# All tiles at multiples of 64 bytes in a partition, and projection pieces of 432, 448 or 480 columns

## The chip, the core and the metric

The kernel runs on one core of a Trainium2 chip. The time is what the device takes for one execution of the whole program, in microseconds (us); lower is better. TensorE (PE in the profile) multiplies, with its weight loads listed apart as PEld; VectorE (DVE), ScalarE (ACT) and GpSimd (POOL) do the rest, and SyncE (SP) issues the DMAs.

## What is computed

Two transformer blocks of two layers each, over 256 tokens with 1024 features, in float32:

```
for l in range(2):      # first block
    x = x + 0.5 * swiglu(rms_norm(x, ffn1_norm[l]), w_gate, w_up, w_down)     # 1024 -> 2816 -> 1024
    h = rms_norm(x, mix_norm[l])
    proj = h @ w_in[l]                       # split: GLA, FOX attention, SSD, short convolution
    x = x + concatenate([gla, fox, ssd, sconv]) @ w_out[l]
    x = x + 0.5 * swiglu(rms_norm(x, ffn2_norm[l]), ...)
for l in range(2):      # second block: the same, but
    proj = h @ w_in_2[l]                     # split: NSA (compressed, selected, window) and MOBA heads
    x = x + concatenate([o_nsa, o_moba]) @ w_out_2[l]
return rms_norm(x, norm_final_2)
```

## The kernel before

**Precision.** Every dense product is made of float32r products: each operand is split exactly into a first and a second part (`hi`, `lo` of a weight, `xhi`, `xlo` of the tokens), and three of the four partial products are summed in PSUM. `weights` (L320 to L335) loads a piece of a weight matrix into a tile `raw`, ACT copies it into `hi` (L332), DVE subtracts (L333) and writes `lo`.

**Which operand streams.** A product has a stationary operand, loaded by LDWEIGHTS, and a moving one, whose columns stream past it. There are four kinds of dense product.

- `gemm_T` (feed-forward gate and up, and projection pieces that come out transposed): stationary are 128 columns of `hi` or `lo`, moving is `xs`, the tokens' two parts side by side. For each 128 columns there is one matmul of 512 columns (`hi`) and one of 256 (`lo`), in two PSUM banks in turn.
- Feed-forward down, in `ffn`: the same pair of 512 and 256 columns, but moving is a tile `hT` (22 of them, made by L524 and L525), in four PSUM banks in turn.
- `w_out`: three matmuls of 256 columns, moving `yhi`, `ylo`, `yhi`.
- `project`: tokens as rows. Stationary are 128 columns of `xs`, moving is a row of the weight piece, `hi`, `lo` and `hi` again through `mm3`; so each piece has twice as many `hi` as `lo` products. Its pieces are 436, 434 and 434 columns wide in the first block (`W1`) and six times 474 in the second (`W2`). With 8 blocks of features, 2 halves of the tokens and 3 products, a piece is 48 matmuls.

**Order.** A phase of feed-forward runs its pieces one after the other. In a mixing phase `drive` puts the mixers' small float32 products and transposes between the dense products: it keeps a clock `self.clk`, which `mm` moves on by columns / 2400 (four times that for float32), and a mixer goes on when that clock has reached the time at which it expects its input. So the width of a piece enters the order in which TensorE's instructions are written. `pieces` asks for a piece's weights one piece ahead.

**Where tiles lie.** The pools place tiles one after another in each partition, every tile at the next multiple of 32 bytes. In the built program these are the starts modulo 64 bytes:

```
tile                      before                         after
x, xs, cst (ident)        0                              0
raw, hi, lo               32                             0
hT, g, h, sq, ss          32                             0
yhi, ylo                  32 in mix1, 0 in mix2          0
pj                        32                             0
s2, sm, p, pT             32 in mix1, 0 in mix2 (sm: both)   0
row k of hi, lo in project:
  436 columns             32, 48, 0, 16                  0 (448 columns)
  434 columns             32, 40, 48, 56                 0 (432 columns)
  474 columns             32, 8, 48, 24                  0 (480 or 448 columns)
```

The tile `gf` of 32 bytes is what puts the pools behind it at 32; `prm`, `ms` and `r` and the rows of `pj` (1304 and 2844 floats for each half of the tokens) shift others.

Of the kernel before, what the change touches and what calls it, by code (L numbers as in the profile page):

```python
# [21 lines left out]
# widths of the pieces in which the input projections are computed  # L22
# with tokens as rows; the other columns come out transposed, 256 at a time
W1 = [436, 434, 434]
W2 = [474] * 6
IN1, IN2 = sum(W1), sum(W2)
NB1 = 9
# NSA heads in the order that pairs a head of group 0 with one of group 1
POS = [0, 4, 1, 5, 2, 6, 3, 7]

# [20 lines left out]
def _consts():  # L51
    """Masks, triangles and rope tables: they depend on shapes alone."""
# [38 lines left out]
def _pack(widths, w):  # L91
    """[1024, sum(widths)] -> flat, one [128, 8, width] block after the other."""
    w = w.reshape(8, 128, -1).transpose(1, 0, 2)
    out, o = [], 0
    for n in widths:
        out.append(w[:, :, o:o + n].reshape(-1))
        o += n
    return np.concatenate(out)
# [6 lines left out]
def layout(inp):  # L105
    """Lays the inputs out for the chip: slices, transposes, copies."""
    a = {k: np.asarray(v) for k, v in inp.items()}
    f32 = np.float32
# [11 lines left out]
    for l in range(2):  # L120
# [9 lines left out]
        out[f"wi{l}"] = _pack(W1, np.concatenate([lr, bf, cdt, bq, bk, bv, av, ag], 1))  # L130
# [66 lines left out]
class Body:  # L197
# [5 lines left out]
    def run(self, ctx, phases, final):  # L203
# [10 lines left out]
        # x transposed, in two halves of the features: [128, (block of 128 features, token)]  # L214
        self.x = [self.cst.tile([128, 4, 256], F32, name=f"x{n}") for n in range(2)]
        C = self.cst.tile([128, CW], F32, name="cst")
# [6 lines left out]
        # keeps the array busy, and its clock up, until the first operands are there  # L223
# [22 lines left out]
        self.gf = self.cst.tile([128, 8], F32, name="gf")  # L246
# [47 lines left out]
    def params(self, ph, cut=None):  # L294
        """Loads a block's parameters, in two parts if asked to: then returns the second's load."""
        key = ph[2], ph[3]
        if key in self.pars:
            return
        fields, w = (_P1, PW1) if ph[2] == "p1" else (_P2, PW2)
        p, src = self.prm.tile([128, max(PW1, PW2)], F32, name="prm"), self.a[f"{ph[2]}_{ph[3]}"]  # L300
        self.pars[key] = {n: p[:, o:o + k] for n, (o, k) in fields.items()}
        self.nc.sync.dma_start(p[:, :cut or w], src[:, :cut or w])
        return lambda: self.nc.sync.dma_start(p[:, cut:w], src[:, cut:w])
# [14 lines left out]
    def weights(self, src, nk, n, parts=1, then=None):  # L318
        """A piece of a weight matrix and its exact split into two float32r parts."""
# [34 lines left out]
    def behind(self):  # L354
        """Matrix products traced in it are issued behind the dense ones traced so far."""
        return self.tc.issue_after(self.last_mm) if self.last_mm is not None else nullcontext()

    def drive(self, dense, mixers):
        """Interleaves the dense products with the mixers' steps. A generator yields before a product
        that has to wait: how much of other products to put before it, the name of what it needs, or  # L360
        "@" for one of the places among the attentions in progress."""
# [28 lines left out]
    def rrow(self, pool, r):  # L390
        """r [128 tokens, 2] as a row over the 256 tokens, on every partition."""
# [9 lines left out]
    def norm(self, k):  # L401
        """A block of 128 features of x times the next norm's gain, split in two."""
# [5 lines left out]
    def sumsq(self, n):  # L408
        """Sums of x's squares over half the features, but for the sum over the partitions."""
# [13 lines left out]
    def rfin(self):  # L423
        """(mean of x's squares + eps) ** -0.5: [128 tokens, 2]"""
        nc = self.nc
        ms = self.wk.tile([128, 2], F32, name="ms")
        r = self.wk.tile([128, 2], F32, name="r")
# [9 lines left out]
    def x_done(self, n):  # L437
        """Half of x's features are final."""
        if self.nxt:
            self.sumsq(n)  # L440

    def x_last(self, n, b):
        """A block of the last x: its squares join the sums; turned to tokens as rows by a product with
        the last norm's gains on a diagonal."""
# [22 lines left out]
    def gemm_T(self, ps, ws, k):  # L467
        """256 columns of a weight matrix, through 128 of its rows: in PSUM, for each block of 128 columns,
        the products with the tokens' first and second parts side by side."""
# [8 lines left out]
    def evac_T(self, out, ps, R, eng):  # L478
        """out [128, 2 * 256] = the sums of the parts, times the tokens' factors."""
# [78 lines left out]
    def pieces(self, make):  # L558
        """Runs the dense pieces, each a pair (load, run); a piece's weights are asked for one ahead."""
# [7 lines left out]
    def project(self, w, widths, c, half, box):  # L567
        """Half of the rows of a piece of the projection with tokens as rows."""
# [24 lines left out]
    def project_T(self, w, c, R, box):  # L593
        """256 columns of the projection, transposed: box[c] [128, 512] = (block of 128, token)."""
# [13 lines left out]
    def w_out(self, i, kq, n, box, last):  # L608
        """x += y @ w_out, through the rows kq of w_out, for half the columns."""
# [37 lines left out]
    def finish(self, y, k0, nk, g):  # L647
        """Columns of y [128, 2, nk * 128] into the transposed, split operand of w_out."""
# [13 lines left out]
    def rms(self, y, n, d, scale=1.0, eps=EPS):  # L662
        """(mean of squares over the last d + eps) ** -0.5 of y [128, n * d] -> [128, n]."""
# [15 lines left out]
    def sigm(self, out, x):  # L679
        """1 / (1 + exp(-x)) = exp(-ln(1 + exp(-x)))"""  # L680
# [5 lines left out]
    def attn2(self, qT, kT, v, po, first=True, last=True, guard=True, gate=None):  # L686
        """Two heads' causal softmax(q k) v over 256 tokens, transposed, onto po [2 * 64, 256] in PSUM.
        qT[h], kT[h]: [d, 256], one of them negated; v[h][t]: [128, 64]; gate: [128, (h, t)] factors of the rows."""
# [40 lines left out]
    def pv2(self, po, v, a, b, first, last):  # L729
        """po [2 * 64, 256] += v[h]^T P[h]^T; a: keys 0..127 by (h, 256 queries), b: keys 128.. by  # L730
        (h, the last 128 queries)."""
# [7 lines left out]
    def finish_T(self, y, k0, n, mat, d, src=None, wait=2.5):  # L739
        """rms norm over d rows of the transposed y [128, n * 256] (PSUM src, else in place), with the  # L740
        gains, into the split operand of w_out."""
# [12 lines left out]
        # one Newton step for the root  # L754
# [44 lines left out]
    def logs(self):  # L799
        """log-sigmoids: of GLA's gate and FOX's forget logit, and -softplus of SSD's step."""  # L800
# [33 lines left out]
    def gla(self, c0, B):  # L834
        """c0: columns of v and the output gate in pj; B[0], B[1]: transposed q and k."""
# [24 lines left out]
        # v of each head, zero in the columns of the pair's other head  # L860
# [79 lines left out]
    def fox(self, c0):  # L940
# [21 lines left out]
        # the running sums of the log forget gates, next to q and k  # L962
# [39 lines left out]
    def conv(self, x, acc, j, taps, bias):  # L1002
        """acc[:, j] = causal convolution of x[:, j] along the tokens; taps[-1] is the newest."""
# [117 lines left out]
    def compress(self, l):  # L1121
        nc, P, pj, C = self.nc, self.P, self.pj, self.C
        mm = self.mm
        # the windows of k and v plus their positions, transposed: [(parity, d), (l / 2, g, n)]
# [32 lines left out]
        # hidden = window @ w1: four partial sums, on four groups of 32 partitions (g, n)  # L1157
# [61 lines left out]
    def pairT(self, c, n, dst, scale=None):  # L1219
        """n blocks of 128 columns of pj from c, transposed to [128, 256] each."""  # L1220
# [42 lines left out]
    def nsa_cmp(self):  # L1263
        """The compressed branch: all heads at once, columns (head, n)."""
# [34 lines left out]
    def nsa_pair(self, p):  # L1299
        """The compressed branch's values, and the selected and window branches: over 256 tokens both see  # L1300
        all that is not in the future."""
# [61 lines left out]
```

## Time and profile before

| | us |
|---|---|
| median of 3 runs (lowest, highest) | 2036.2 (2035.51, 2037.14) |
| profiled execution, span from its first to its last instruction | 2034.5 |
| TensorE busy in it | 2017.6 |
| VectorE, ScalarE, GpSimd busy | 1623.0, 1226.2, 417.8 |

No other time of the profiled execution is recorded than its span, which lies 1.7 us under the median. Matmuls are pipelined and their ends are modelled, so TensorE's busy share says little of its pace. The pace is read from the starts: the time from one matmul's start to the next one's, or a stretch of the chain of waits that is TensorE alone, divided by its count of matmuls.

### The profile page before, as it was taken

What the parts mean: (1) busy time and instruction counts of PE and PEld (TensorE: products, weight loads), DVE (VectorE), ACT (ScalarE), POOL (GpSimd) and SP (SyncE); (2) the same over time, 40 slices, a digit from 0 to 9 for tenths busy, and PEclk for the clock granted to TensorE, in tenths of its full rate; (3) what the DMA queues carried; (4) which work ended last, traced back from release to release, by engine and by line L of the source; (5) the groups of instructions that cost most, each with busy time, mean ns of one, the idle gap of its engine ahead of it and who ended that gap; (6) DMA issues with size and microseconds to landing.
All of it is one profiled execution on the core that took longest, in us unless ns stands there. A gap on an engine that the chain in (4) does not pass through costs nothing.

```text
span 2034.5 us, 32098 instructions
## 1 busy us (share of the span) xinstructions
PE 2017.6 (99%) x12052; PEld 1769.3 (87%) x12052; DVE 1623.0 (80%) x3140; ACT 1226.2 (60%) x2711; POOL 417.8 (21%) x313
## 2 busy tenths in 40 slices
PE   9999999999999999999999999999999999999998
PEld 7888889888888888988888887898888888789887
DVE  7976888995897688899589766889868976688974
ACT  6655666664665566666466545766556654566653
POOL 2320121330221013132022111023203211103320
PEclk9999999999999999999999999999999999999999
DMA  7655425555555542655555556255555555624552
GB/s 277 210 195 175 155 87 200 198 184 194 190 187 181 197 143 73 221 197 184 192 192 188 181 190 216 80 170 194 187 194 186 187 185 180 217 84 173 194 182 73
DMA packets 54300, 360.88 MB, mean 177 GB/s; under 512 B 6272, under 2 KB 6656, under 8 KB 16768
## 3 DMA queue, kind: packets, MB, share of 16 engines
q1 hardware_dynamic: 54144, 358.83, 50.7%
q8 instruction: 94, 1.54, 0.3%
q14 instruction: 62, 0.51, 0.1%
HBM read 357.76 MB, written 1.05 MB: 176 GB/s over the span
## 4 chain that ended last, share of the span: by engine, by line
PE 92%; issue 3%; DVE 3%; ACT 1%; POOL 0%; DMA 0%; DVEq 0%; POOLq 0%; SPq 0%
PE ps L343 90%; PE ps L347 2%; DVE lo L333 1%; DVE s L1011 1%; DVE xs L405 0%; ACT p L703 0%; DMA raw<-gu 0%; DVE x L633 0%; POOL s L1023 0%; PE ps L395 0%; PE ps L431 0%; ACT hi L332 0%; DVE p L701 0%; POOL g L486 0%; DVE s L756 0%
## 5 line engine op out<-in xcount | busy, mean ns | idle before, releaser
L333 DVE TENSOR_TENSOR lo<-raw,hi 128x512 fp32r<-128x512 f32 (+2 forms) x1336 | 1059.1, 824 | 233.7 <-ACT hi L332 220.2
L343 PE MATMUL ps<-xs,hi 128*128 128x512 f32 x3104 | 1088.2, 393 | 3.4 <-DVE xs L405 3.4
L332 ACT ACTIVATE hi<-raw 128x512 fp32r<-128x512 f32 (+2 forms) x1336 | 751.3, 620 | 270.4 <-PE ps L343 147.3
L343 PE MATMUL ps<-xs,lo 128*128 128x256 f32 x3104 | 875.7, 282 | 0.9 <-DVE lo L333 0.9
L343 PEld LDWEIGHTS ps<-xs,hi 128*128 128x128 f32 x3104 | 584.6, 188 | 126.5 <-DVE xs L405 3.9
L343 PEld LDWEIGHTS ps<-xs,lo 128*128 128x128 f32 x3104 | 588.0, 190 | 2.7 <-DVE lo L333 1.6
L343 PE MATMUL ps<-hT,hi 128*128 128x512 f32 x1408 | 494.7, 393 | 0.0
L486 POOL TENSOR_TENSOR g<-g,R 128x512 f32<-128x512 f32 x176 | 296.1, 1684 | 635.3 <-DVE g L484 614.8
L343 PE MATMUL ps<-hT,lo 128*128 128x256 f32 x1408 | 398.2, 283 | 0.0
L343 PEld LDWEIGHTS ps<-hT,hi 128*128 128x128 f32 x1408 | 264.4, 188 | 61.1
L343 PEld LDWEIGHTS ps<-hT,lo 128*128 128x128 f32 x1408 | 264.7, 188 | 0.0
L484 DVE TENSOR_TENSOR g<-ps,g 128x256 f32<-128x256 f32 x352 | 147.3, 421 | 63.3 <-ACT g L483 63.2
L483 ACT ACTIVATE g<-ps 128x256 f32<-128x256 f32 x352 | 132.9, 379 | 91.6 <-PE ps L343 91.3
L343 PE MATMUL ps<-hi,xs 128*128 128x474 f32 (+2 forms) x576 | 182.0, 381 | 0.0
L522 ACT ACTIVATE h<-g 128x256 f32<-128x256 f32 x176 | 73.7, 419 | 178.5 <-POOL g L486 178.4
L524 ACT ACTIVATE hT<-h 128x256 fp32r<-128x256 f32 x176 | 73.3, 418 | 82.2 <-DVE h L523 82.2
L343 PEld LDWEIGHTS ps<-hi,xs 128*128 128x128 f32 x576 | 108.0, 188 | 14.6 <-issue 2.3
L343 PE MATMUL ps<-lo,xs 128*128 128x474 f32 (+2 forms) x288 | 107.2, 372 | 0.0
L523 DVE TENSOR_TENSOR h<-h,g 128x256 f32<-128x256 f32 x176 | 78.3, 447 | 15.3 <-ACT h L522 15.3
L415 POOL TENSOR_TENSOR sq<-sq 128x512 f32<-128x512 f32 x12 | 18.4, 1534 | 324.7 <-ACT sq L414 324.7
L434 POOL TENSOR_TENSOR r<-ms,cst 128x2 f32<-128x2 f32 x13 | 11.2, 862 | 328.6 <-DVE ms L433 328.6
L525 DVE TENSOR_TENSOR hT<-h,hT 128x256 fp32r<-128x256 f32 x176 | 73.4, 419 | 1.9 <-ACT hT L524 1.9
(214 smaller groups left out, 1540.5 us busy)
## 6 DMA issues: line engine op xcount, KB each, us to landing
raw<-gu SPq DMA_DIRECT2D x174, 1024.0 KB, 4.8
raw<-wd SPq DMA_DIRECT2D x80, 1024.0 KB, 4.8
raw<-wj SPq DMA_DIRECT2D x24, 948.0 KB, 4.8
raw<-wb SPq DMA_DIRECT2D x18, 1024.0 KB, 4.8
raw<-wo SPq DMA_DIRECT2D x12, 1024.0 KB, 5.0
raw<-wd SPq DMA_DIRECT2D x16, 512.0 KB, 3.3
raw<-cw SPq DMA_DIRECT2D x8, 1024.0 KB, 4.9
raw<-wi SPq DMA_DIRECT2D x8, 868.0 KB, 4.5
```

What stands on the lines that cost most here:

```text
L332: nc.scalar.activation(hi[:, c], raw[:, c], AF.Copy)
L333: nc.vector.tensor_tensor(lo[:, c], raw[:, c], hi[:, c].bitcast(F32), op=OP.subtract)
L343: return self.nc.tensor.matmul(out, w, x, **kw)
L347: self.nc.tensor.transpose(out, x, self.ident)
L483: nc.scalar.activation(o, ps[b][:, 256:512], AF.Copy)
L484: nc.vector.tensor_tensor(o, ps[b][:, 0:256], o, op=OP.add)
L486: eng.tensor_tensor(o2, o2, R[:, None, :].to_broadcast([128, 2, 256]), op=OP.mult)
L522: self.last_silu = nc.scalar.activation(h, g[:, 0:256], AF.Silu).ins
L523: nc.vector.tensor_tensor(h, h, g[:, 256:512], op=OP.mult)
L524: nc.scalar.activation(hT[c][:, 0], h, AF.Copy)
L525: nc.vector.tensor_tensor(hT[c][:, 1], h, hT[c][:, 0].bitcast(F32), op=OP.subtract)
L1011: nc.vector.scalar_tensor_tensor(a[:, s:], p[:, :256 - s], taps[len(taps) - 1 - s], a[:, s:], op0=OP.mult, op1=OP.add)
```

## The change

Widths are rounded so that every tile, and every row of a weight piece in `project`, starts at a multiple of 64 bytes. The zero columns at the end (8 in `W1`, 4 more than before in `W2`) are multiplied like the others and written to `pj`, where nobody reads them. All comments and docstrings are gone as well, so line numbers are lower or higher by a few (L343 becomes L350).

```diff
-W1 = [436, 434, 434]
-W2 = [474] * 6
+W1 = [448, 432, 432]
+W2 = [480] * 5 + [448]
+def _up(n):
+    return -(-n // 16) * 16
...
-        out[f"wi{l}"] = _pack(W1, np.concatenate([lr, bf, cdt, bq, bk, bv, av, ag], 1))
+        pad = np.zeros((DM, IN1 - 1304), f32)
+        out[f"wi{l}"] = _pack(W1, np.concatenate([lr, bf, cdt, bq, bk, bv, av, ag, pad], 1))
...
-        C = self.cst.tile([128, CW], F32, name="cst")
+        C = self.cst.tile([128, _up(CW)], F32, name="cst")
...
-        self.gf = self.cst.tile([128, 8], F32, name="gf")
+        self.gf = self.cst.tile([128, 16], F32, name="gf")[:, :8]
...
-        p, src = self.prm.tile([128, max(PW1, PW2)], F32, name="prm"), self.a[f"{ph[2]}_{ph[3]}"]
+        p, src = self.prm.tile([128, _up(max(PW1, PW2))], F32, name="prm"), self.a[f"{ph[2]}_{ph[3]}"]
...
-        ms = self.wk.tile([128, 2], F32, name="ms")
-        r = self.wk.tile([128, 2], F32, name="r")
+        ms = self.wk.tile([128, 16], F32, name="ms")[:, :2]
+        r = self.wk.tile([128, 16], F32, name="r")[:, :2]
```

In the feed-forward phases no instruction moves. In `mix2` the other widths shift `drive`'s clock, and TensorE's order changes in some places. The first is in the compressed branch, where `raw` and `s` are its products with the window weights, `cst,pj` are transposes, and `hi,xs` and `lo,xs` the projection. Before:

```order
L343 MATMUL ps<-hi,xs 128x474
L343 MATMUL ps<-raw,s_12354 32x256 x8
L347 MATMUL ps<-cst,pj 128x128 x8
L343 MATMUL ps<-cst,s_12422 128x128 x4
L343 MATMUL ps<-hi,xs 128x474
```

After, on TensorE at the same place:

```order
L350 MATMUL ps<-raw,s_12351 32x256 x8
L350 MATMUL ps<-hi,xs 128x480
L350 MATMUL ps<-lo,xs 128x480
L350 MATMUL ps<-hi,xs 128x480
L350 MATMUL ps<-cst,s_12413 128x128 x4
L350 MATMUL ps<-hi,xs 128x480
L350 MATMUL ps<-lo,xs 128x480
L350 MATMUL ps<-hi,xs 128x480 x2
L350 MATMUL ps<-lo,xs 128x480
L350 MATMUL ps<-hi,xs 128x480
L354 MATMUL ps<-cst,pj 128x128 x8
```

One group of float32 work between two dense products has become three. The second place is the transposes of the attention's probabilities `p` in the last projection piece. Before:

```order
L343 MATMUL ps<-hi,xs 128x474
L347 MATMUL ps<-cst,p 128x128
L343 MATMUL ps<-lo,xs 128x474
L347 MATMUL ps<-cst,p 128x128 x5
L343 MATMUL ps<-hi,xs 128x474 x2
```

After, on TensorE at the same place:

```order
L350 MATMUL ps<-hi,xs 128x448
L350 MATMUL ps<-lo,xs 128x448
L354 MATMUL ps<-cst,p 128x128 x4
L350 MATMUL ps<-hi,xs 128x448
L354 MATMUL ps<-cst,p 128x128 x2
```

The dense products between the transposes stand one product later. Over the whole program the dense and the other products follow one another, change of kind counted, 284 times before and 292 times after.

## Rows read from the trace of the kernel before

**Rows 1.** The page: busy time of TensorE, the granted clock in 40 slices, and the shares of the chain of waits by engine.

```profile
PE 2017.6 (99%) x12052; PEld 1769.3 (87%) x12052; DVE 1623.0 (80%) x3140; ACT 1226.2 (60%) x2711; POOL 417.8 (21%) x313
...
PEclk9999999999999999999999999999999999999999
...
PE 92%; issue 3%; DVE 3%; ACT 1%; POOL 0%; DMA 0%; DVEq 0%; POOLq 0%; SPq 0%
```

**Rows 2.** The longest waits of TensorE: who waited for whom, us in total, times, longest.

```profile
PE ps L343 <- POOL s L1023: 5.4, 2, 2.7
PE ps L343 <- DVE xs L405: 3.4, 1, 3.4
...
PE ps L343 <- DVE lo L333: 0.9, 2, 0.5
```

**Rows 3.** The chain of waits in the first feed-forward phase, once in its gate and up products (`gemm_T`), once in its down products: start, length, instructions.

```profile
23.29 110.82 PE ps L343 x639
...
134.11 61.56 PE ps L343 x351
```

**Rows 4.** Instructions of TensorE in order of time, in the gate and up products: start and length in us.

```profile
60.23 0.39 PE L343 MATMUL ps<-xs,hi 128*128 128x512 f32 x1
60.45 0.28 PE L343 MATMUL ps<-xs,lo 128*128 128x256 f32 x1
...
61.27 0.39 PE L343 MATMUL ps<-xs,hi 128*128 128x512 f32 x1
```

**Rows 5.** The same in the down products; the rows left out are their `lo` products.

```profile
139.68 0.40 PE L343 MATMUL ps<-hT,hi 128*128 128x512 f32 x1
...
140.03 0.39 PE L343 MATMUL ps<-hT,hi 128*128 128x512 f32 x1
...
140.38 0.40 PE L343 MATMUL ps<-hT,hi 128*128 128x512 f32 x1
...
140.73 0.40 PE L343 MATMUL ps<-hT,hi 128*128 128x512 f32 x1
...
141.09 0.39 PE L343 MATMUL ps<-hT,hi 128*128 128x512 f32 x1
```

**Rows 6.** The same in `w_out`, first in `mix1`, then in `mix2`; between the two rows of each lie eight matmuls of 256 columns.

```profile
318.52 0.28 PE L343 MATMUL ps<-ylo,hi 128*128 128x256 f32 x1
...
319.58 0.28 PE L343 MATMUL ps<-ylo,hi 128*128 128x256 f32 x1
...
1330.23 0.28 PE L343 MATMUL ps<-ylo,hi 128*128 128x256 f32 x1
...
1331.31 0.28 PE L343 MATMUL ps<-ylo,hi 128*128 128x256 f32 x1
```

**Rows 7.** The same in `project`, at a width of 434 and of 474; between the two rows of each lie eleven matmuls.

```profile
209.10 0.36 PE L343 MATMUL ps<-lo,xs 128*128 128x434 f32 x1
...
211.48 0.36 PE L343 MATMUL ps<-lo,xs 128*128 128x434 f32 x1
...
1246.07 0.38 PE L343 MATMUL ps<-lo,xs 128*128 128x474 f32 x1
...
1248.66 0.37 PE L343 MATMUL ps<-lo,xs 128*128 128x474 f32 x1
```

**Rows 8.** Groups of TensorE instructions by shape: count, busy us, mean ns of one, idle time before them. PEld rows are weight loads, of `hi` at 32 bytes and of `xs` at 0.

```profile
L343 PE MATMUL ps<-xs,hi 128*128 128x512 f32 x3104 | 1088.2, 393 | 3.4 <-DVE xs L405 3.4
...
L343 PEld LDWEIGHTS ps<-xs,hi 128*128 128x128 f32 x3104 | 584.6, 188 | 126.5 <-DVE xs L405 3.9 <-issue 1.2
L343 PE MATMUL ps<-hT,hi 128*128 128x512 f32 x1408 | 494.7, 393 | 0.0
...
L343 PE MATMUL ps<-hi,xs 128*128 128x474 f32 x384 | 125.9, 389 | 0.0
L343 PEld LDWEIGHTS ps<-hi,xs 128*128 128x128 f32 x576 | 108.0, 188 | 14.6 <-issue 2.3
...
L343 PE MATMUL ps<-hi,xs 128*128 128x434 f32 x128 | 37.7, 365 | 0.0
```

**Rows 9.** One VectorE operation of the attention, on `p`, by shape: in the first layer's `mix1` (195 to 331 us) and `mix2` (1212 to 1346 us).

```profile
L714 DVE TENSOR_SCALAR p<-p,sm 128x256 f32<-128x256 f32 x4 | 1.4, 346 | 0.0
...
L714 DVE TENSOR_SCALAR p<-p,sm 128x256 f32<-128x256 f32 x24 | 8.7, 362 | 0.3
```

**Rows 10.** TensorE in order of time around one group of float32 products in `mix2`.

```profile
1230.30 0.37 PE L343 MATMUL ps<-hi,xs 128*128 128x474 f32 x1
1230.60 1.07 PE L343 MATMUL ps<-raw,s 128*32 128x256 f32 x16
1231.60 0.49 PE L343 MATMUL ps<-hi,xs 128*128 128x474 f32 x1
1231.93 0.38 PE L343 MATMUL ps<-lo,xs 128*128 128x474 f32 x1
```

**Rows 11.** The chain of waits in `mix1` from 251 to 272 us: two of its longest pieces, and its last.

```profile
260.69 2.70 DVE s L1011 x5
...
264.10 2.41 DVE lo L333 x4
...
269.73 2.39 POOL s L1023
```

## The prediction

> **What bounds the kernel now.** I read the page first. TensorE is busy 99% of the span, its granted clock is in the top tenth in all 40 slices (the upper level, 2.4 GHz), and the chain of waits is TensorE for 92% [rows 1]. A reader might stop there, but ends of matmuls are modelled, so the next view is TensorE's waits: beyond 3.4 us at the start there are two of up to 2.7 us in `mix1` and two of 0.5 us [rows 2]. Hardly 10 us of 2034.5 are waits, so only two things can move the time: the pace at which products follow one another, and the order in which kinds of product follow.
>
> The pace is read from starts. In gate and up, 639 matmuls of the chain take 110.82 us, 173.4 ns each [rows 3]. Half have 512 columns, half 256, on average 384, which at 2.4 GHz is 160.0; so 13.4 ns come on top. In down, the same pair of shapes takes 61.56 us for 351, or 175.4 ns, 15.4 on top [rows 3]. The timelines say the same: three pairs in 1.04 us, or 347 a pair [rows 4], against four pairs in 1.41, or 352 [rows 5]. What differs is the tile that streams, `xs` at 0 or `hT` at 32 modulo 64. `w_out` in `mix2`, moving tile at 0, needs 1.08 us for nine matmuls, 120.0 each, 13.3 over its 256 columns' 106.7; in `mix1`, moving tile at 32, 1.06 us, 117.8 [rows 6]. In `project`, twelve matmuls of 434 columns take 2.38 us, 198.3 each, 17.5 over 180.8; of 474 columns 2.59 us, 215.8, or 18.3 over 197.5 [rows 7]. So streams whose moving tile begins at 0 lose 13.3 ns a matmul, twice over; those whose rows begin at 8, 24, 40 or 56 lose 17.5 to 18.3. Between lies a start at 32, with 15.4 in one place and 11.1 in the other.
>
> **The change part by part.** *Down.* 1408 `hi` products [rows 8] and as many `lo` get a moving tile at 0. I take gate and up's pace, the row with the same shapes: 2816 x (175.4 - 173.4) = **-5.5 us**. Its bounds are nothing, if the 2 ns come from down's four PSUM banks or its shorter accumulations, and -8.2 by the pairs of the two timelines, (352.5 - 346.7) / 2 = 2.9 ns a matmul, whose starts are rounded to 0.01 us.
>
> *Projection.* At columns / 2.4 + 13.3 the new widths would take 193.3 (432), 200.0 (448) and 213.3 ns (480). One layer's 434 pieces are 96 matmuls, so 192 x (193.3 - 198.3) = -0.96; 436 to 448, for which I take 199.1 (435 columns or so at 17.5 over), 96 x 0.9 = +0.1; five pieces 474 to 480, 480 x (213.3 - 215.8) = -1.2; the last piece 474 to 448, 96 x (200.0 - 215.8) = -1.5. Together -3.6. But the last `W1` piece lies under the chain of VectorE and GpSimd that ends in the 2.7 us wait [rows 2, 11]: what TensorE saves there it waits for longer. That takes back 0.48: **-3.1 us**. If start addresses do nothing, only the columns count: 96 x 12 - 192 x 2 + 480 x 6 - 96 x 26 = 1152 columns, / 2.4 = +0.5 us.
>
> *`w_out` in `mix1`.* Here 32 was the faster row. 384 matmuls x (120.0 - 117.8) = +0.85; two waits for `lo` of 0.5 us [rows 2] lie near and can take part of it: **+0.5 us**, between 0 and +0.9. `w_out` in `mix2` begins at 0 already: nothing.
>
> *Order in `mix2`.* Four more groups of float32 work between dense products, four fewer direct joints of float32 work and transposes (284 changes of kind, then 292). What a detour costs: the last dense product ahead starts 0.30 us before the group rather than 0.216, and the first one behind it needs 0.33 us to the next start rather than 0.216 [rows 10], so 0.2 us in all. Four of these cost 0.8, and the joints that vanish give part back, which no row here prices: **+0.4 us**, between -0.5 and +1.2. The transposes of `p` stand a product later. What covers that is that TensorE has other products in front of it; without the cover, a wait of 0.4 to 0.6 us per layer would show, and the upper bound has room for one.
>
> *The other engines.* A VectorE operation on `p` took 346 ns with the tile at 32 and 362 at 0 [rows 9], so alignment gains nothing there; if the 16 ns were the alignment's, the four of a `mix1` would lose 0.06 us beside TensorE's work. The DMAs carry under 1% more for the projections (8 columns on 1304, 4 on 2844), one piece ahead: nothing. Where a GpSimd or VectorE piece ends the chain [rows 11], I take its length as unchanged.
>
> The sum: -5.5 - 3.1 + 0.5 + 0.4 = **-7.7 us** on a span of 2034.5, so 2026.8; the median of the runs stands 1.7 above that span, so **2028.5**. With the terms' bounds, this case's own range is 2024 to 2032.
>
> One rule speaks against the change. The rows show 173.4 and 175.4 ns for a mean of 384 columns. The Trainium skill, "TensorE: Matmul & The Clock Gate", section "Back-to-back issue gap", gives an isolated gap of columns / 2.4 + 2.5 ns at full clock, which knows no address: an estimate from it is 162.5 for both streams, lower than either row. By it alone the change would only add the columns' 0.5 us. The trace disagrees with its constant (13.3 here), so I keep to the rows.
>
> **The rivals.** *Equal remainders collide; slower.* Gate and up are now 0 (moving) against 32 (weights); down is 32 against 32, and it is the slower one. If what costs 2 ns is that stationary and moving tile have the same remainder, then the change puts 3104 x 2 products of gate and up [rows 8] on that footing: 6208 x 1.95 = +12.1, down stays, columns +0.5, order +0.4, projections as they were: 2036.2 + 13.0 = **2049**. For it: down is the only stream of pairs with equal remainders. Against it: `w_out` in `mix1`, 32 against 32, is faster than in `mix2`, 0 against 32 [rows 6]. It decides from the first pair of gate and up: 347 or 351 ns.
>
> *Addresses do nothing that is worth the name.* Down is slower for its four PSUM banks, project for its short pieces. Then what is left is columns and order, +0.5 + 0.4: **2037**. For it: down and gate and up differ in more than an address, and `w_out` contradicts the sign [rows 6]. Against it: project's 17.5 to 18.3 ns on top of its columns stand against 13.3 and 13.4 in two unlike products that stream from 0 [rows 3, 6, 7]. A finer grid is a variant: project's rows at 8, 24, 40 and 56 gain, 32 costs nothing. Then -3.1 + 0.4, so 2033.5, still inside 0.2%. The Trainium skill, "SBUF — State Buffer", section "Door 1: The DMA port swizzle", in its note on cachelines, says that SBUF's lines are 16 bytes and that each access that crosses to a new line pays. By that rule, 32 is as good a start as 0, down would gain nothing and only project's pieces would, which is this variant; [rows 3] and [rows 7] bear it out for project, not for down.
>
> *The weights' start counts as well; a larger gain.* `hi` and `lo` go from 32 to 0 in all of gate, up, down and `w_out`. If that alone brings 2 ns on the 6208 + 2816 + 768 of these, it is -19.6 us; with the rest of the sum, **2009**. Against it: a weight load takes 188 ns for `hi` at 32 as for `xs` at 0 [rows 8], and project, with weights at 0, is the slowest stream over its columns [rows 7].
>
> **How the numbers follow.** Forecast 0.58, equal remainders 0.18, addresses nothing 0.17 with its variant, the larger gain 0.07. A change of 0.2%, 4.1 us, is about what a measurement of this kernel can tell from none. The forecast's range reaches from 12 us under the median to 4 under it, so nearly all of it is faster; with the larger gain, and a little less for the variant's lower edge, faster has 0.62. Addresses doing nothing, the forecast's upper edge and an equal-remainders price cut to a third give same 0.21; equal remainders in full give slower 0.17. Faster holds most of the chance; its own range is 2024 to 2032. For 8 in 10 the larger gain is left out and the slower rival must be in: **2022 to 2050**.
>
> **What would show it.** In the changed kernel's profile: down's pairs every 347 ns rather than 352; gate and up still 173.4 ns a matmul; `w_out` in `mix1` at 120 and not 118; project at about 193, 200 and 213 ns for its three widths; the wait on GpSimd's `s` in `mix1` longer by 0.2 us a layer; four more groups of float32 products in `mix2`, each costing 0.2 us. The forecast is wrong if gate and up move at all (upwards: equal remainders; downwards: the weights' start), if down stays at 352 with `hT` at 0, or if a new wait of TensorE above 1 us shows in `mix2`.

## The result, and the profile after

| | us |
|---|---|
| before, median of 4 runs | 2036.67 |
| after, median of 4 runs (lowest, highest) | 2059.56 (2059.34, 2061.14) |
| ratio, 95% interval | 1.0115 [1.0104, 1.0127] |
| profiled execution's span, before and after | 2034.5, 2057.6 |

The change makes the kernel slower by 23 us, where 7.7 us of gain were forecast. The page after has the same rows as [rows 1]:

```profile
PE 2040.6 (99%) x12052; PEld 1764.6 (86%) x12052; DVE 1621.9 (79%) x3140; ACT 1226.5 (60%) x2711; POOL 418.6 (20%) x313
...
PEclk9999999999999999999999999999999999999999
...
PE 91%; issue 4%; DVE 3%; ACT 1%; POOL 0%; DMA 0%; SPq 0%; DVEq 0%; POOLq 0%
```

TensorE is busy for as many instructions, 23.0 us longer, with the granted clock in the top tenth of all 40 slices again (its mean is 0.999, and was 0.997 before); the other engines stay within 2 us. So the 23 us are no clock, and the chain of waits has hardly changed. The longest waits of TensorE show that they are no wait either, against [rows 2]:

```profile
PE ps L350 <- POOL s L1030: 5.8, 2, 2.9
PE ps L350 <- DVE xs L412: 3.1, 3, 1.4
```

Next is the pace. The chain of waits in the first feed-forward phase, in gate and up and in down (start, length, instructions), against [rows 3]:

```profile
22.24 110.82 PE ps L350 x627
...
135.30 61.71 PE ps L350 x349
```

The 110.82 us that held 639 matmuls before hold 627 now: 176.7 ns each, not 173.4. Down went from 175.4 to 176.8. The timelines show which of the two shapes it is. First gate and up (three pairs between the two rows), then down (four pairs), against [rows 4, 5]:

```profile
60.23 0.40 PE L350 MATMUL ps<-xs,hi 128*128 128x512 f32 x1
60.47 0.28 PE L350 MATMUL ps<-xs,lo 128*128 128x256 f32 x1
...
61.29 0.40 PE L350 MATMUL ps<-xs,hi 128*128 128x512 f32 x1
...
139.37 0.40 PE L350 MATMUL ps<-hT,hi 128*128 128x512 f32 x1
...
140.78 0.40 PE L350 MATMUL ps<-hT,hi 128*128 128x512 f32 x1
```

A pair takes 353 ns in both, where gate and up had 347. (Down's four pairs show the same 1.41 us as before, since these starts are rounded to 0.01 us; its change is read from the chain.) The next start comes 0.24 us behind a 512-column product, where it was 0.22; the 256-column product still takes 0.12. The other two dense products, in the timeline: `w_out` in `mix1` (33 matmuls between the rows), then `project` at 432 (12), 448 (27) and 480 columns (9), against [rows 6, 7]:

```profile
316.97 0.28 PE L350 MATMUL ps<-ylo,hi 128*128 128x256 f32 x1
...
320.92 0.28 PE L350 MATMUL ps<-ylo,hi 128*128 128x256 f32 x1
...
210.02 0.35 PE L350 MATMUL ps<-lo,xs 128*128 128x432 f32 x1
...
212.38 0.36 PE L350 MATMUL ps<-lo,xs 128*128 128x432 f32 x1
...
197.51 0.37 PE L350 MATMUL ps<-lo,xs 128*128 128x448 f32 x1
...
202.92 0.36 PE L350 MATMUL ps<-lo,xs 128*128 128x448 f32 x1
...
1253.75 0.38 PE L350 MATMUL ps<-lo,xs 128*128 128x480 f32 x1
...
1255.70 0.38 PE L350 MATMUL ps<-lo,xs 128*128 128x480 f32 x1
```

That is 119.7 ns in `w_out`, and 196.7, 200.4 and 216.7 ns in `project`. The account, with paces from all starts that no wait disturbs: gate and up 6208 x (176.66 - 173.33) = +20.7; down 2816 x (176.6 - 175.5) = +3.1; `w_out` in `mix1` 384 x 2.1 = +0.8; the projections' products, from start to start and their joints with other work among them, 190.6 us before and 191.2 after, +0.6. That is 25.2; 1.0 us comes back where the first long stretch of gate and up begins (at 22.24 and not 23.29 us). In the first 15 us the granted clock was 0.77 in the execution profiled before and 1.00 in the one after, so no row here makes that 1.0 us an effect of the change. The last us is spread.

### The profile page after: what moved, and what is told of

It is laid out like the page before. It is cut to its first block, busy times and chain, and to the rows that moved or that the text cites. A ratio compares the mean times of both kernels' runs of the same rounds, so it can differ in the third digit from the quotient of the medians.

```text
span 2057.6 us, 32098 instructions
## 1 busy us (share of the span) xinstructions
PE 2040.6 (99%) x12052; PEld 1764.6 (86%) x12052; DVE 1621.9 (79%) x3140; ACT 1226.5 (60%) x2711; POOL 418.6 (20%) x313
## 4 chain that ended last, share of the span: by engine, by line
PE 91%; issue 4%; DVE 3%; ACT 1%; POOL 0%; DMA 0%; SPq 0%; DVEq 0%; POOLq 0%
PE ps L350 89%; PE ps L354 2%; DVE lo L340 1%; DVE s L1018 1%; DVE xs L412 0%; ACT p L710 0%; DMA raw<-gu 0%; DVE x L640 0%; POOL s L1030 0%; ACT hi L339 0%; PE ps L402 0%; PE ps L438 0%; DVE p L708 0%; DVE pj L594 0%; DVE p L721 0%
## 5 line engine op out<-in xcount | busy, mean ns | idle before, releaser
L350 PE MATMUL ps<-xs,hi 128*128 128x512 f32 x3104 | 1105.3, 399 | 3.1 <-DVE xs L412 3.1
L350 PE MATMUL ps<-xs,lo 128*128 128x256 f32 x3104 | 871.8, 281 | 0.6 <-DVE lo L340 0.6
L350 PEld LDWEIGHTS ps<-xs,hi 128*128 128x128 f32 x3104 | 584.0, 188 | 147.0 <-DVE xs L412 4.6
L350 PEld LDWEIGHTS ps<-xs,lo 128*128 128x128 f32 x3104 | 583.1, 188 | 2.3 <-DVE lo L340 1.2
L350 PE MATMUL ps<-hT,hi 128*128 128x512 f32 x1408 | 497.8, 399 | 0.0
L350 PE MATMUL ps<-hT,lo 128*128 128x256 f32 x1408 | 395.5, 281 | 0.0
L350 PEld LDWEIGHTS ps<-hT,hi 128*128 128x128 f32 x1408 | 264.6, 188 | 65.9
L350 PEld LDWEIGHTS ps<-hT,lo 128*128 128x128 f32 x1408 | 266.0, 189 | 0.0
L350 PE MATMUL ps<-hi,xs 128*128 128x480 f32 (+2 forms) x576 | 182.2, 380 | 0.0
L350 PEld LDWEIGHTS ps<-hi,xs 128*128 128x128 f32 x576 | 108.2, 188 | 15.2 <-issue 3.1
L350 PE MATMUL ps<-lo,xs 128*128 128x480 f32 (+2 forms) x288 | 107.3, 373 | 0.0
L422 POOL TENSOR_TENSOR sq<-sq 128x512 f32<-128x512 f32 x12 | 18.3, 1528 | 326.1 <-ACT sq L421 326.1
```

The source lines that it names most:

```text
L350: return self.nc.tensor.matmul(out, w, x, **kw)
```

## The experiments

Ratios are against the kernel before, with the intervals of the same runs. The number in parentheses after a label is the median of its runs, or the one time where it was run once.

### Widths alone, tiles alone, one line undone

`widths_only` is the kernel before with `W1 = [448, 432, 432]` and `W2 = [480] * 5 + [448]`; `tiles_only` is the changed kernel with the old widths.

> The kernel before with the new widths of the projection pieces alone; every tile starts where it did. Theory A (the 23 us come from the start of the weight tiles, 32 before and 0 after, modulo 64, because gate and up went from 173.33 to 176.66 ns a matmul): gate and up stay at 173.3 ns, down at 175.5, and the time is 2036.7 with at most 2 us either way for columns, order and the pieces' row starts. Theory B (the widths, or the order in mix2 that follows from them, cost a good part): above 2042.

> The changed kernel with the old widths of 436, 434 and 474 columns; hi, lo, hT and xs start at 0. Theory A: gate and up at 176.7 ns and down at 176.6, so 2036.7 + 20.7 + 3.0 and 0.8 for w_out in mix1, about 2061. Theory B: gate and up may be at 176.7, but the time stays below 2055.

```diff
-        self.gf = self.cst.tile([128, 16], F32, name="gf")[:, :8]     # weights_at_32
+        self.gf = self.cst.tile([128, 8], F32, name="gf")
```

> The changed kernel with one line undone: gf is 32 bytes wide again, so raw, hi, lo and hT start at 32 modulo 64 (hi and lo at 32 modulo 128, where the kernel before had 96), xs stays at 0 and the new widths stay. Theory A: gate and up back at 173.3 ns, down at 175.5, time 2036 to 2037. Theory C (what counts is not the start modulo 64 but one place of the weights against xs on a coarser grid, as the distance to xs changed by 96 bytes in all): gate and up at neither 173.3 nor back to it, time above 2042.

`widths_only` (2039.75, 1.0016 [1.0007, 1.0025]): gate and up at 173.3, down at 175.4. The chain of its first phase:

```profile
22.73 110.59 PE ps L343 x638
...
133.90 60.15 PE ps L343 x343
```

`tiles_only` (2055.96, 1.0099 [1.0086, 1.0113]): 176.6 and 176.8. So the tiles' places bring the loss and the widths and the order a small one beside it; theory B falls. Widths alone took 3.4 us more than the kernel before in the same runs (2036.33), a little beyond the 2 us that theory A left for them. Of the 2.2 us by which the span grew, 2.0 are in the projections' starts (192.6 us for 190.6). Tiles alone came out 5 us under its expectation; a part is `w_out` in `mix1`, at 113.6 ns here (33 matmuls in 3.75 us), which no theory so far had:

```profile
319.02 0.28 PE L350 MATMUL ps<-ylo,hi 128*128 128x256 f32 x1
...
322.77 0.28 PE L350 MATMUL ps<-ylo,hi 128*128 128x256 f32 x1
```

`weights_at_32` (2055.11, 1.0095 [1.008, 1.011]): theory A falls. Weights and `hT` start at 32 modulo 64 as before, and most of the loss stays. In the profiled execution (2049.2 us, the fastest of four, 2049.2 to 2056.05) gate and up have two paces at one and the same address; the chain in the first and in the fourth feed-forward phase:

```profile
23.09 110.13 PE ps L350 x635
...
848.20 110.82 PE ps L350 x627
```

173.4 and 176.7 ns: five of the eight phases have the lower pace, and the fourth, sixth and eighth the higher. Down is at 176.7 in all eight.

### A sweep of both starts

```diff
+        self.xs = ... tile([128, 8, 520]) ...       # a block of xs every 2080 bytes; hT likewise
+        oh, ol = 8 * (self.nw % 4), 8 * (self.nw % 4)      # nw: number of the weight piece
+        hi = self.hip.tile([128, 2080], F32R, name="hi", tag="hi")[:, oh:oh + 2048]
```

> The changed kernel with starts that vary within the run: the eight blocks of xs stand 32 bytes further each (0 to 224 modulo 256), the 22 tiles hT too, and hi and lo of each next weight piece begin 0, 32, 64 or 96 bytes into their tile. Read is the time from a 512-column matmul's start to the next start, by moving start and weight start. Theory A1 (equal remainders modulo 64 of moving and weights are slow): 235 ns wherever the two are equal modulo 64, also at 32 against 32, and 228 elsewhere, so that about half of all are slow. Theory A2 (weights at a multiple of 64 are slow whatever streams): 235 wherever the weights are at 0 modulo 64, 228 where they are at 32. Theory C: the table follows modulo 128 or 256, and no grid of 64 orders it.

`sweep` (2046.21). Mean ns from a 512-column product of gate and up to the next start, by the start of its `xs` block and of the weights loaded next, both modulo 256:

```
xs \ weights     0     32     64     96    128    160    192    224
   0         234.4  232.1  232.0  230.7  233.2  232.9  231.3  229.8
  64         233.7  229.2  236.2  232.4  233.1  234.1  230.6  231.8
 128         231.5  232.8  229.1  229.3  236.7  231.3  236.3  234.9
 192         236.0  235.0  229.7  232.8  229.5  229.1  236.5  231.5
```

On the diagonal it is slow. But 0 and 128 or 128 and 64, equal modulo 64, are not as slow (233.2 and 229.1), so A1 falls, and weights at a multiple of 64 run at 229 as well as at 236, so A2 falls. What recurs in every row is a distance, by which is meant from here on the weights' start less the moving operand's start, modulo 256: weights 32 bytes ahead of the moving start (to the left of the diagonal, a distance of 224) take 229.1 to 229.8, and equal starts 234.4 to 236.7. It does not order the whole table: at a distance of 64 the four rows give 232.0 to 236.3, at 192 they give 229.1 to 233.7. Seen so, the old paces can be set beside their distances. Gate and up before: `xs` at 0 and weights at 224 modulo 256, a distance of 224; after, 64. Down: 96 and 224, a distance of 128; after, `hT` and weights both at 64, 0. In `weights_at_32` 32 and 0.

### Distances, each held for a piece or for a run

```diff
-        self.gf = self.cst.tile([128, 16], F32, name="gf")[:, :8]     # aligned_distance_192
+        self.gf = self.cst.tile([128, 48], F32, name="gf")[:, :8]
+            fp.tile([128, 16], F32, name="gap")                        # ahead of hT
```

> The changed kernel, every tile still at a multiple of 64, but raw, hi and lo 128 bytes further (gf takes 192 bytes) and hT 64 bytes further still: the weights begin 192 bytes after the start of the moving tile, counted modulo 256, in gate and up and in down, where the changed kernel has 64 and 0. Theory D (what counts is the distance from the moving start to the weights' start modulo 256, as the sweep's table says: 229 ns for a 512-column product at a distance of 192 or 224, 235 to 237 at 0 and 64): gate and up 173.3 ns a matmul, down 173.3 too, so 2059.6 - 20.7 - 9.2, about 2030, faster than the kernel before. Theory A (starts modulo 64, equal or at 0): gate and up stay at 176.7, down at 176.6, time about 2059.

Measured 2061.72, 1.0119 [1.0102, 1.0136]: not the gain expected. The chain of its first phase, gate and up and then down:

```profile
22.57 110.47 PE ps L350 x625
...
136.00 60.06 PE ps L350 x340
```

176.8 and 176.6 ns. The price that I read from the sweep was wrong: of its four values at a distance of 192 only two were near 229, and there the products next to each other have other distances, where the last experiments show that what comes before counts. Both stages now have the same pace, but `xs` and `hT` both begin at 0 and the weights at 192 modulo 256, so this run does not tell a distance from an address. What does comes below: `sweep_4_bytes`, and `w_out` in two kernels. The table of distances had to be taken at a steady stream.

```diff
+        oh, ol = 4 * (self.nw % 32), 4 * (self.nw % 32)               # sweep_16_bytes
+        oh, ol = 48 + self.nw % 32, 48 + self.nw % 32                 # sweep_4_bytes
+        oh, ol = 8 * (self.nw % 8), 8 * (self.nw // 8 % 8)            # hi_lo_apart
```

> The changed kernel with three raw buffers instead of four, and hi and lo of each next weight piece beginning 16 bytes further, 0 to 496; xs and hT stay. Theory D: a piece of gate and up runs at 173.3 or at 176.7 ns by the distance, slow in a band of distances from 0 to about 96 modulo 256, the same in both halves of the 512 bytes. Theory A: slow at every fourth step, fast at the three between.

> As the sweep by 16 bytes, but in steps of 4 bytes from 256 to 380 modulo 512 of the first start (distance 0 to 124 modulo 256). Theory D: no fine structure; what 16-byte steps show holds between them. A rival (starts off a 16- or 32-byte grid cost more): slower by at least 3 ns where the start is no multiple of 16 or 32.

> The changed kernel with three raw buffers, hi and lo of a piece shifted apart: hi by 0 to 224 bytes in steps of 32, lo by as much in a slower cycle. Read is a piece's time for a pair of 512 and 256 columns by both distances. Theory D1 (the load that runs beside the 512-column product counts, and that is the load of lo): the pair is slow by the distance of lo alone, whatever hi's is. Theory D2 (both loads count, or the hi load before the product): the table changes along hi's distance too.

`sweep_16_bytes` (2047.39). The timeline of two neighbouring pieces of gate and up, at a distance of 48 (15 pairs between the first two rows) and of 64 (14 pairs):

```profile
95.46 0.40 PE L352 MATMUL ps<-xs,hi 128*128 128x512 f32 x1
...
100.66 0.39 PE L352 MATMUL ps<-xs,hi 128*128 128x512 f32 x1
...
101.35 0.40 PE L352 MATMUL ps<-xs,hi 128*128 128x512 f32 x1
...
106.30 0.40 PE L352 MATMUL ps<-xs,hi 128*128 128x512 f32 x1
```

The 5.20 us are 346.7 a pair or 173.3 a matmul; the 4.95 us are 353.6 or 176.8. All pieces of this run by distance, ns a matmul; the 8 to 12 gate and up pieces and the 3 to 8 down pieces of a distance agree within 0.6, in both halves of the 512 bytes, but for one or two pieces where two paces stand:

```
  0: 173.2/176.4    64: 176.7   128: 175.5          192: 176.6
 16: 173.3          80: 176.3   144: 174.8          208: 175.0
 32: 173.3          96: 173.3   160: 175.0          224: 173.3
 48: 173.3         112: 176.6   176: 176.7/174.8    240: 176.7/173.3
```

The kernels whose starts stay fixed lie on it at four distances: 224 at 173.3, 128 at 175.5, 64 at 176.7, 192 at 176.7. They do not at 0: down ran at 176.6 to 176.8 in all eight phases of the changed kernel, `tiles_only` and `weights_at_32`, and in the sweep 15 pieces of 16 ran at 173.2. So it is at 32: 173.3 here, about 176.3 in `sweep_4_bytes`, both paces in `weights_at_32`. Some distances, then, have two paces. Theory A predicted every fourth step slow and the others fast; nothing of the kind. The band of D is wrong too: it is a pattern that has to be looked up. Among the multiples of 64 none is always at 173.3, which is how a change that puts all tiles on them comes out slow.

`sweep_4_bytes` (2048.97): D's "no fine structure" falls, paces go from 173.3 at 44 to about 182 at 60 bytes; and so does its rival, since 24, 44 and 84 run at 173.3 and the multiple of 16 at 64 at 176.7. Here `xs` begins at 0 and `hT` at 64 modulo 256, so that one distance stands for unlike addresses in gate and up and in down, and yet they have the same pace: about 182 in six undisturbed pieces of six at 60, 176.0 in nine of nine at 36. This is where a distance is told from an address.

`hi_lo_apart` (2045.78): with `lo` at distance 0, `hi` at 0, 32, 64 and 96 gives in gate and up 176.8 or 173.3, 175.6, **170.0** and 173.4. So both starts count, D2. One piece of down had 64 and 0 as well and ran at 175.0, which the next expectation leaves out. The timeline of the piece at 64 and 0, 15 pairs in 5.10 us:

```profile
1412.37 0.39 PE L352 MATMUL ps<-xs,hi 128*128 128x512 f32 x1
...
1417.47 0.39 PE L352 MATMUL ps<-xs,hi 128*128 128x512 f32 x1
```

### All tiles at multiples of 64, and faster

```diff
+        self.rawp, self.hip, gap, self.lop = pool("raw", 4), pool("hi", 3), pool("gap", 1), pool("lo", 3)
+        gap.tile([128, 48], F32, name="gap")
```

> The changed kernel, every tile still at a multiple of 64, with 192 empty bytes between the pools hi and lo and nothing else: modulo 256, hi begins 64 bytes and lo 0 bytes after the moving tile, in gate and up, in down (hT moves to 0) and in w_out. Theory D2 (both weight starts count, by their distance to the moving start; the run with hi and lo apart shows 170.0 ns at this pair of distances in both pieces that have it): gate and up 170.0 and down 170.0 ns a matmul, so 2059.6 - 6208 x 6.66 (41.3) - 2816 x 6.6 (18.6) = about 2000, well below the kernel before too; if VectorE or the loads become the bound on the way, up to 2015. Theory A (starts at multiples of 64 are what costs, or equal remainders modulo 64): nothing changes, about 2059.

> As the run with hi and lo apart, in steps of 16 bytes for both, 256 pairs of distances. Theory D2: paces between 170 and 177 ns in steps, 170 near the pair of 64 and 0; perhaps a pair that is faster still. Theory A: 176.7 wherever both are multiples of 64, which the pair of 64 and 0 has already shown otherwise.

`lo_192_further` (2029.97, 0.9969 [0.9958, 0.9981]): 30 us less than the changed kernel for 192 empty bytes, and faster than before, with every tile at a multiple of 64. Alignment to 64 is neither the harm nor the good. It is 30 us short of its expectation, and the chain says why; gate and up in the first and in the third phase:

```profile
22.22 110.84 PE ps L351 x633
...
528.76 107.34 PE ps L351 x631
```

175.1 and 170.1 ns at the same addresses, kept for a whole phase, down included; three phases of eight had 170.0, and its six executions lie between 2026.06 and 2035.35. The three are the third, fifth and seventh, which follow directly on another feed-forward phase; the five at 175.0 follow the start or a mixing phase. `apart_16_bytes` (2042.34) found no faster pair; its 64 and 0, in one piece, ran at 174.9.

### Down's step by itself, and `w_out`

```diff
+            fp.tile([128, 40], F32, name="gap")      # hT_160_further: kernel before, ahead of hT
+            mp.tile([128, 32], F32, name="gap")      # w_out_distance_64: also ahead of yhi in mix1,
+            mp.tile([128, 24], F32, name="gap")      # and in mix2
```

> The kernel before with 160 empty bytes ahead of hT and no other edit: in down the weights now begin 224 bytes after the moving tile modulo 256, as they do in gate and up, instead of 128. Theory D: down takes gate and up's 173.3 ns in place of 175.5, 2816 x 2.2 = 6.2 us, so about 2030, and no other stage changes. The rival that down is slower for its four PSUM banks: 2036.

`hT_160_further` (2029.33, 0.9964 [0.995, 0.9978]), as expected; down in the chain of its first phase:

```profile
133.24 60.79 PE ps L343 x351
```

173.2 ns with all four PSUM banks in use, in each of the eight phases. The banks cost nothing.

> The run with hT 160 bytes further, and yhi and ylo 128 bytes further in mix1 and 96 in mix2, so that in w_out too the weights stand at a chosen distance: 64 bytes after the moving tile modulo 256, in place of 192 and 160. Theory D (distance, for every kind of dense product): w_out as in mix1 of the run with the tiles alone, the one place with a distance of 64, 113.9 ns a matmul in place of 117.8 and 119.9, so 384 x 3.9 + 384 x 6.0 = 3.8 us less, about 2025.5. Its rival (the law holds only for pairs of 512 and 256 columns; that the place ran at 113.9 had another cause): w_out stays at 118 to 120, time 2029.3.

`w_out_distance_64` (2027.34, 0.9954 [0.9941, 0.9968]): `w_out` in the timeline of `mix1` (36 matmuls) and of `mix2` (33):

```profile
313.89 0.28 PE L343 MATMUL ps<-ylo,hi 128*128 128x256 f32 x1
...
317.97 0.28 PE L343 MATMUL ps<-ylo,hi 128*128 128x256 f32 x1
...
1320.07 0.28 PE L343 MATMUL ps<-ylo,hi 128*128 128x256 f32 x1
...
1323.82 0.28 PE L343 MATMUL ps<-ylo,hi 128*128 128x256 f32 x1
```

113.3 and 113.6 ns for 117.8 and 120.0. The starts of `w_out` sum to 90.5 us, where `hT_160_further` had 94.0, and the span fell by 4.0 us to 2024.8, about as worked out; the medians differ by 2.0 only. The third kind of product follows the distance as well: in `mix1` of `tiles_only` the weights stood at 64 and `yhi` at 0 modulo 256, here at 224 and 160. Its table is another than that of the pairs, for which 64 is slow (176.7).

### What settles which of two paces is kept

```diff
+        o = 0 if self.kick else 8                     # both: kick is set for c == 2 alone
+        hi = self.hip.tile([128, 2048 + 64], F32R, name="hi", tag="hi")[:, o:o + 2048]
+        lo = self.lop.tile([128, 2048 + 64], F32R, name="lo", tag="lo")[:, o:o + 2048]   # entry_32_224 only
```

> The run with lo 192 bytes further, and in each feed-forward phase one gate and up piece of 22 (the third) with hi 32 bytes lower, distances 32 and 0; hi stands in tiles with 256 spare bytes for that. That run had 170.0 ns in three phases of eight and 175.0 in five, at the same addresses. Theory E (which of two paces a stretch keeps is settled by the products that come just before it; in the run with hi and lo apart, pieces at 32 and 0 were followed by pieces at 64 and 0 with 170.0): after the third piece all eight phases run at 170.0, gate and up and down, so 2030 - 5 phases x 1032 matmuls x 5 ns = 26, about 2004. Its rival (a phase's pace is set by something else, such as the phase before or the weights' arrival): some phases stay at or return to 175.0, and the time to about 2030.

`other_entry` (2050.73, 1.0069 [1.0056, 1.0082]): the opposite of the gain expected. No phase reached 170.0; five ran at 175.0 and three at 176.7. The chain of the first two:

```profile
22.77 110.26 PE ps L355 x630
...
343.29 111.84 PE ps L355 x633
```

I had misread which piece came ahead of the 170.0 in `hi_lo_apart`: it had distances of 32 and 224, not 32 and 0. A piece at 32 and 0 stood ahead of the one that ran at 175.0.

> The run of the other entry, with the third piece of each feed-forward phase 32 bytes lower in lo as well as in hi: distances 32 and 224 there, 64 and 0 in all other pieces; three raw buffers in place of four make the room. Before the two gate and up pieces that ran at 170.0 in the run with hi and lo apart stood a piece at 32 and 224, and before the one in down that ran at 175.0 a piece at 32 and 0, as in the other entry; so that run set the slower of the two. Theory E (what comes just before settles which pace is kept): from the fourth piece on all eight phases run at 170.0, about 2004, with 5 us either way for w_out's changed distance. Its rival (something else settles it): some or all phases at 175.0 or 176.7, 2025 to 2055.

`entry_32_224` (2007.8, 0.9856 [0.984, 0.9873]) is the fastest version. The chain in its first two phases, from the fourth piece of gate and up on, with nearly all of down:

```profile
28.38 159.69 PE ps L355 x939
...
344.43 159.57 PE ps L355 x939
```

170.1 and 169.9 ns. From the fourth piece on all eight phases of the profiled execution run at 170.0, whatever came before the third. So behind a single piece of 32 products at other addresses the thousand that follow keep one pace, as theory E said. This run and `other_entry` differ in more than `lo` of that piece: it also has three raw buffers, and 32 bytes ahead of `hT`. The number of buffers alone does not settle the pace, for 170.0 and 175.0 both occurred with four (`lo_192_further`) and with three (`hi_lo_apart`); a run with three and no other entry was not made.

## Why the prediction was wrong, point by point

**What bounds the kernel** was read rightly: pace and order, not waits.

**The step that failed** stands ahead of the terms for the dense products: "What differs is the tile that streams, `xs` at 0 or `hT` at 32 modulo 64". As a rule for a stream's pace it gave down a gain of 5.5 us, which came out as a loss of 3.1, and gate and up nothing, which came out as a loss of 20.7.

**Down**: the rule enters with "I take gate and up's pace, the row with the same shapes". It put the 2 ns down to the moving tile's start modulo 64. The runs showed in its place the distance from the moving start to the starts of `hi` and `lo`, modulo 256: 128 in down and 224 in gate and up before. Where the distance is made 224, down does take gate and up's pace, and the -5.5 us measure -5.7 by spans (2034.5 to 2028.8) and -7.3 by the ratio of 0.9964 (`hT_160_further`). The change made the distance 0 and the pace 176.6, +3.1 us.

**Gate and up**, put at nothing, are 20.7 of the 23 us. The forecast held them fixed because the start of `xs` did not move. What stood ahead of it moved: the weights went from 224 to 64. Of the weights' start I had only weighed a gain.

**Projection**: forecast 193, 200 and 213 ns, measured 196.7, 200.4 and 216.7; the paces alone give -1.2 and not -3.6, and the starts of the projections' products, joints with other work among them, grew by 0.6 in all. "Columns / 2.4 + 13.3" was no constant of a start at 0, and the 17.5 to 18.3 of the old widths were means over rows that begin at 32 and 48 as well as at 8, 24, 40 and 56. **`w_out` in `mix1`**, +0.5 forecast, is +0.8: the right size from the wrong cause, for the same multiple of 64 runs at 113.6 in `tiles_only`. **The wait on GpSimd's `s`** grew by 0.2 us a layer, as said. **Order in `mix2`** shows in `widths_only`: of the 2.0 us by which the projections' starts grow the paces explain 0.6, which leaves 1.4 for joints with other work, a little above the term's upper bound of 1.2. The count of groups was short: 284 and 292 are changes between three kinds, dense products, float32 products and transposes. From dense to other work and back there are 254 changes before and 266 after, which is six more groups, four of float32 products and two of transposes. At 0.2 us each they cost 1.2, where the prediction had four.

**The rivals.** Equal remainders had the sign, and its point of decision (351 ns a pair in gate and up) was passed: 353. Its mechanism falls, in `weights_at_32` and in `lo_192_further`, and its 12 us for gate and up were 20.7. Its counter-evidence, `w_out` faster at 32 against 32, was sound: it spoke against every account by remainders of 64, mine too, and I let it count against the rival alone. That addresses do nothing falls with `tiles_only`, which has the old widths and loses 20 us. That the weights' start counts as well was right, but the gain of 19.6 us had the wrong sign.

**Still open** is why a distance costs what it does. That a load of the next weights and the stream get in each other's way fits that both starts and what ran before count, but no run here took the loads away; this is argued, not shown. A rival to it, that other engines or the DMAs get in TensorE's way in SBUF, is answered by the changed kernel's trace. Near its end down runs for 2.6 us in which VectorE, ScalarE, GpSimd and the DMAs do nothing. The first row has the window, its length, the busy time of PE, PEld, DVE, ACT and POOL, the granted clock, and the DMAs' share and GB/s; between the other two lie six pairs:

```profile
2039.60:2042.20 2.60, 2.60 (x17) 2.22 (x16) 0.00 (x0) 0.00 (x0) 0.00 (x0) 1.00 0.00 0
...
2039.82 0.40 PE L350 MATMUL ps<-hT,hi 128*128 128x512 f32 x1
...
2041.94 0.40 PE L350 MATMUL ps<-hT,hi 128*128 128x512 f32 x1
```

2.12 us are 353 ns a pair, as everywhere in down: the loss is there without any of them.

## What to carry to other kernels

Write down whole addresses of both operands, and their differences, before a pace is put down to an alignment: here two tiles that only had a remainder in common were taken for the cause. A stream that is never interrupted can have several paces for the same instructions, so measure the pace a stage long, by starts, after every change of layout, even by a small tile far off. Once known, it is cheap to use: 192 empty bytes were worth 30 us on the changed kernel, and with one piece at other distances near the head of each feed-forward phase as well, 2036 became 2008.

## What the runs showed of the hardware that was not expected

- The time from one float32r product to the next depends on where both operands lie, with the granted clock at its upper level but for a few short stretches (mean 0.995 to 1.0): 170.0 to about 182 ns for the pair's mean of 384 columns, 113.3 to 120.0 for 256. That is 10 to 22 ns over the 160.0 of 384 columns, and 6.6 to 13.3 over the 106.7 of 256.
- It repeats modulo 256 bytes of distance (`sweep_16_bytes` went over 512), and at one distance it is the same for `xs` and `hT`, two banks or four (`sweep_4_bytes`, `hT_160_further`), but for distances such as 0 and 32, which have two paces.
- It has a memory: the same addresses kept 170.0 or 175.0 ns for a thousand products, and in the runs here the pace went with what ran just before.
- The Trainium skill, "TensorE: Matmul & The Clock Gate", section "Back-to-back issue gap", has a constant of 2.5 ns over the columns at full clock for an isolated gap; by it a matmul of these pairs would take 162.5. The section itself sets that gap apart from a stream of weight loads and products, where both set the spacing. No stage here came under 170.0, so the constant is no guide for this stream.
- The Trainium skill, "SBUF — State Buffer", section "Door 1: The DMA port swizzle", says that each access that crosses to a new 16-byte line pays a penalty. No such step shows here: distances of 44 and 48 bytes both gave 173.3, and the line-aligned 64 gave 176.7.
